# A hybrid decoder layer on one core: the output projection of the first 1024 tokens as eight tiles in a PSUM bank of its own, written out and read back by the norms

## The chip, the cores and the metric

The kernel runs on one core of a Trainium2 chip. The metric is the device time of one launch in microseconds (us): the median of several runs. A profile is one further execution, recorded instruction by instruction; all rows below come from it. The engines are PE (TensorE: matmuls, transposes as matmuls with an identity, and, as PEld, weight loads that overlap them), DVE (VectorE), ACT (ScalarE), POOL (GpSimd) and SP (SyncE, which here only issues DMAs). SBUF is the memory on the core, DRAM the memory outside; PSUM is PE's output memory, eight banks of 128 x 512 f32, which DVE and ACT read ("drain").

## The reference

One layer of a decoder for a prompt of 2048 tokens (width D = 1024) and 32 sample tokens. Cut to what matters here:

```
xn = rmsnorm(x);  [u|q k v f|z xBC dt|B C h] = xn @ W_in
ya = S5(u)        yb = fox attention(q,k,v,f)     # 4 heads x 64, causal, with forget bias
yc = SSD(z,xBC,dt) # Mamba-2, 4 heads, 16 chunks of 128 tokens, a state carried from chunk to chunk
yd = short conv(B,C,h)                            # each of the four is 256 wide and RMS-normed
x  = x + concat(ya,yb,yc,yd) @ W_out              # the output projection
x  = x + relu(rmsnorm(x) @ W_up)^2 @ W_down       # the FFN, 4096 wide
y  = rmsnorm(x)
```

## The kernel before

**Tiles.** The 2048 tokens are four blocks of 512, grouped as `BLOCKS=[(2,3),(0,1)]`: the FFN takes blocks 2 and 3 first and keeps blocks 0 and 1 (the first 1024 tokens) in DRAM until then. Products that need more precision than f16 gives are done three times with high and low f16 halves: x is split into hi and lo, and hi·hi, hi·lo and lo·hi are summed in one PSUM bank.

**The order of the work.** The program is written with a framework that simulates each engine's time line, and by that and by priorities puts all instructions into one fixed list for each engine; the engines run their lists in order, and semaphores make an instruction wait for its inputs or for a free buffer. So an instruction that waits holds up all that stands behind it in its engine's list. Written order is: the input projections (`phase_in`), SSD (`ssd`), attention (`fox`, with another priority, so that its instructions fill in beside SSD), output projection (`outproj`), FFN (`ffn`). In the trace attention's score exponentials run from 746 to 1132 us, SSD's chunks from about 856 to 1048, the output projection's matmuls from 1061 on, and the FFN follows.

**Attention** (`fox`). For each of the four blocks j and each head h, `maxima` makes scores to find the row maxima (tiles `kbm`, `mx`), some steps ahead, and `attend` goes over the 128-key tiles: scores by two matmuls into a "b" bank (`pb<-q,k` and `pb<-q,kba`; the kba and kbm tiles come from DRAM), an exponential on ACT (`P`, L902), its f16 copy on ACT for three tiles of four (`ph`, L906), the remainder on POOL (`pl`), then three matmuls with v for each 128 queries ("AV"), summed in a bank that the head keeps. After the last head of a block `fox_out` norms 128 tokens at a time: a square on ACT (`fo_on`, `fo_ssq`, L956), a scaled copy on ACT (L959), two transposes, and copies to `fo_cat`, which are written to DRAM as the attention quarter of `catD`.

**SSD** (`ssd_prompt`). Sixteen chunks, each with `prepare` (one chunk ahead) and `advance`. Small products through "x" and "d" banks, an exponential `sE`, copies `sBt`, and DVE work between them. After chunks 10, 12, 13 and 14 one fourth of W_out is prepared (`w_out`, `wprep`): 1 MB loaded into `ws`, a square over it on ACT (`wscale`), a scaled f16 copy on ACT and the low half on DVE (`split`).

**PSUM.** One pool of eight banks: two "x", one "d", five "b". Scores and AV go to "b"; SSD uses "x" and "d"; the output projection uses "x" for its products (`px`) and "d" for the norms' transposes (`pd`).

**Output projection** (`outproj`). It goes over pairs of 128-token tiles, 256 tokens each. `load` brings the normed quarters (`cat`, four DMAs, two buffers) and x (1 MB into `x2`). `product` makes 128 tokens x 512 columns by 48 matmuls (128 x 256 each) in an "x" bank, and two DVE instructions (L1907) add it to x2. For blocks 0 and 1 each of four pairs is loaded, gets its eight products of 24 matmuls, and `norm_pair` follows at once: a square on ACT (`xn`), a multiplication on DVE, eight transposes a tile through the one "d" bank, their copies on ACT (`xt`), and `combine`: differences on DVE (`tt`), then f16 hi on ACT and lo on DVE (`hnr`). x2 and hnr are written to DRAM (`xD`, `hD`), from where the FFN takes them later. Then block 2 is loaded and projected (`first`), the pools of attention are closed, block 2's norms follow, and block 3.

Blocks 2's and 3's x2 and those of blocks 0 and 1 share the same two x2 tiles, with one buffer each, so block 2's x can only be loaded when the norms of the pair that was in its tile have read it.

Of the kernel before, what the change touches and what calls it, by code (L numbers as in the profile page):

```python
# [9 lines left out]
F32 = mybir.dt.float32  # L10
F16 = mybir.dt.float16
# [3 lines left out]
OP = mybir.AluOpType  # L15
# [4 lines left out]
D = 1024  # L20
# [7 lines left out]
BLOCKS = [(2, 3), (0, 1)]  # L28
# [75 lines left out]
class K:  # L104
# [29 lines left out]

    def ps(self, tag, shape, name=None, dt=F32):
        g = self.bank.get(tag, "d" if tag == "w" else tag)
        return self.psum.tile(shape, dt, name=name or ("p" + g), tag=g, bufs={"x": 2, "d": 1, "b": 5}[g])

    def mm(self, out, lhsT, rhs, start=True, stop=True):
        self.nc.tensor.matmul(out, lhsT, rhs, start=start, stop=stop, skip_group_check=True)  # L140
# [95 lines left out]
    def run(self):  # L236
        tc = self.tc
        with ExitStack() as ctx:
            self.consts = ctx.enter_context(self.pool("consts", 1))
            self.small = ctx.enter_context(self.pool("small", 2))  # L240
            self.dr = ctx.enter_context(tc.tile_pool(name="dr", bufs=1, space=bass.MemoryType.DRAM))
            self.psum = ctx.enter_context(tc.tile_pool(name="psum", bufs=1, space=bass.MemoryType.PSUM))
            mix = ctx.enter_context(ExitStack())
            self.mixc = mix.enter_context(self.pool("mixc", 1, "right"))
            with ExitStack() as c2:
                bg = self.phase_in(c2)
            self.wst = ctx.enter_context(self.pool("wst", 2))
            self.wp = ctx.enter_context(self.pool("wp", 4))
            first = tc.cur_priority
            tc.cur_priority = first + 50000  # L250
            if "ssd" in self.stages:
                with self.priority(first), self.banks(t="x", s="x", o="d"), ExitStack() as c3:
                    self.mark("ssd")
                    self.ssd(c3)
            if "fox" in self.stages:
                with self.priority(bg):
                    self.mark("fox")
                    self.fox(mix)
            if getattr(self, "dump", None):
                self.dump_cat()  # L260
            with self.banks(mm="x", t="d"):
                self.mark("out")
                self.outproj(ctx, mix)
            if "ffn" in self.stages:
                self.mark("ffn")
                with self.banks(s="x", mm="b", t="d", o="d"):
                    self.ffn()
# [779 lines left out]
    def ssd_prompt(self, ctx, Dp, av, sample):  # L1047


        nc, tc, A, O = self.nc, self.tc, self.A, self.O  # L1050
# [33 lines left out]
        r = p1.tile([15, 640], F32, name="RLc")  # L1084
# [76 lines left out]
        for i in range(NT):  # L1161
            cur, nx = nx, prepare(i + 1) if i + 1 < NT else None
            old = yo
            hT, yo = advance(i, hT, *cur)

            if old is not None:
                self.fox_out(p2, old, 128, i - 1, "t", 2)
            next(sample, None)
            if i in (10, 12, 13, 14):
                next(wo)  # L1170
        for _ in sample:
            pass
# [1 line left out]
        t = self.ps("t", [128, 2, 128])  # L1174
# [105 lines left out]
    def fox_sample(self):  # L1280
# [3 lines left out]
        with ExitStack() as ctx:  # L1284
# [43 lines left out]
            for hp in range(2):  # L1328
                for hf in range(2):
                    ps = slice(hf * 64, hf * 64 + 64)  # L1330
                    nc.vector.tensor_scalar(Qn[ps, hp, 2 * hp + hf, :], p[ps, hp, :], 0.125, None, op0=OP.mult)
# [417 lines left out]
    def s5_scan(self, p1, p2, XS, Pr, Pi, g0, fin):  # L1749
# [7 lines left out]
        for Q, P in ((Qr, Pr), (Qi, Pi)):  # L1757
            for par in range(2):
                ps = slice(par * 64, par * 64 + 64)
                nc.vector.tensor_copy(Q[ps, :, 1], P[ps, par:8:2, 16])  # L1760
# [107 lines left out]
    def w_out(self):  # L1868
        for m in range(4):
# [4 lines left out]
            self.Wo.append((w, f))  # L1874
            yield

    def outproj(self, ctx, mix):

        nc, A = self.nc, self.A
        W = self.Wo  # L1880
        self.fp = ctx.enter_context(self.pool("ffn", 1))
        self.hnp = ctx.enter_context(self.pool("hn0", 1))
        gb, self.ish, g8 = self.gain_row(self.hnp, A["norm_ffn_g"], "ffn", True)

        self.xp = {BLOCKS[0][0]: ctx.enter_context(self.pool("x2a", 1))}
        rot = mix.enter_context(self.pool("rot", 2, "right"))

        self.xD = {b: [self.dr.tile([128, 2 * D], F32, name=f"x2D{b}{i}") for i in range(2)] for b in BLOCKS[1]}
        self.hD = {b: [self.dr.tile([128, 7 * 4 * 2 * 128], F16, name=f"hnD{b}{i}") for i in range(2)] for b in BLOCKS[1]}

        def load(u, b, i):

            cat = self.hnp.tile([128, 8, 2, 256], F16, name="cat", tag="cat", bufs=2)
            for g in range(4):
                nc.sync.dma_start(cat[:, 2 * g:2 * g + 2], self.catD[g][u // 2][:, :, :, u % 2 * 256:u % 2 * 256 + 256])
            x2 = self.xp[b].tile([128, 2, D], F32, name="x2", tag=f"x2{b}{i}")
            nc.sync.dma_start(x2, A["x_prompt"][0, u * 256:(u + 1) * 256, :].rearrange("(i p) d -> p i d", p=128))
            return cat, x2

        def product(cat, x2, i, m):  # L1900

            p = self.ps("mm", [128, 512])
            for mm in range(2):
                self.proj_tok(p[:, mm * 256:(mm + 1) * 256], cat[:, :, :, i * 128:i * 128 + 128], W[m + mm][0], 0, 256)
            for mm in range(2):
                o = x2[:, i, (m + mm) * 256:(m + mm + 1) * 256]
                nc.vector.scalar_tensor_tensor(o, p[:, mm * 256:(mm + 1) * 256], W[m + mm][1], o, op0=OP.mult, op1=OP.add)  # L1907

        for b in BLOCKS[1]:
            for i in range(2):  # L1910
                cat, x2 = load(2 * b + i, BLOCKS[0][0], i)
                for t in range(2):
                    for m in (0, 2):
                        product(cat, x2, t, m)
                hn = rot.tile([128, 7, 4, 2, 128], F16, name="hnr")
                self.norm_pair(x2, gb, hn)
                nc.sync.dma_start(self.xD[b][i], x2.rearrange("p t d -> p (t d)"))
                nc.sync.dma_start(self.hD[b][i], hn.rearrange("p o k a n -> p (o k a n)"))
        first = [load(2 * BLOCKS[0][0] + i, BLOCKS[0][0], i) for i in range(2)]
        for i, t, m in ((i, t, m) for i in range(2) for t in range(2) for m in (0, 2)):  # L1920
            product(*first[i], t, m)
        mix.close()
        self.xp[BLOCKS[0][1]] = ctx.enter_context(self.pool("x2b", 1, "right"))
        self.hp = ctx.enter_context(self.pool("hn", 1))
        self.bank["t"] = "b"
        self.wup = ctx.enter_context(self.pool("wu", 2, "right"))
        self.wts = {}
        self.accs = self.hp.tile([128, 8, NS], F32, name="accs")
        self.wsc = self.hp.tile([128, 2, 4096 // FC, 2], F32, name="wsc")
        self.x2, self.hn = {}, {}  # L1930
        for b in BLOCKS[0]:
            n = 128 + (NS // 4 if b == BLOCKS[0][0] else 0)
            hn = self.hp.tile([128, 2, 7, 4, 2, n], F16, name=f"hn{b}", tag=f"hn{b}")
            prs = first
            if b != BLOCKS[0][0]:
                prs = [load(2 * b + i, b, i) for i in range(2)]

                for i, t, m in ((i, t, m) for m in (0, 2) for i in range(2) for t in range(2)):
                    product(*prs[i], t, m)
            if b == BLOCKS[0][0]:  # L1940
                self.ffn_wu(0, 0)
            for i in range(2):
                self.norm_pair(prs[i][1], gb, hn[:, i, :, :, :, 0:128], b == BLOCKS[0][1])
            if b == BLOCKS[0][0]:
                self.out_sample(hn, g8)
            self.x2[b] = [x2 for _, x2 in prs]
            self.hn[b] = hn
# [357 lines left out]
```

## Time and profile before

| | us |
|---|---|
| median of 3 runs (2593.56 to 2594.98) | 2594.95 |
| the profiled execution, its own time | 2598.28 |
| its span, from the first instruction to the last | 2596.5 |
| mean granted clock of TensorE, share of full | 0.972 |
| busy: PE / DVE / ACT / POOL | 2439.7 / 2010.8 / 1313.2 / 1212.3 |
| output projection's matmuls `px<-w,cat`, 1536 of them, busy | 180.2 |

All times in rows count from the span's start. A busy time is the union of an engine's instructions; the mean of one matmul is its latency in a pipeline and is longer than the distance from one to the next. Idle time before a group of instructions is followed by what ended it. PEclk is the clock that TensorE was granted, as a share of 2.4 GHz.

### The profile page before, as it was taken

How to read it: one execution, taken by the hardware profiler on the slowest of the kernel's cores; microseconds unless marked ns; L12 is line 12 of the kernel's file. 1: busy time of each engine (PE TensorE's matmuls, PEld its weight loads, DVE VectorE, ACT ScalarE, POOL GpSimd, SP SyncE). 2: the span in 40 equal slices, each digit the busy share in tenths (PEclk: the TensorE clock that was granted, in tenths of full speed). 3: DMA queues.
4: the chain of work that ended last, by engine and by line, in shares of the span. 5: the costliest groups of instructions: out<-in, count | busy, mean ns of one | idle time of the engine just before them, and what ended most of it. 6: DMA issues, size and time to landing. Idle time of an engine off the chain costs nothing.

```text
span 2596.5 us, 51309 instructions
## 1 busy us (share of the span) xinstructions
PE 2439.7 (94%) x20496; PEld 1663.5 (64%) x20496; DVE 2010.8 (77%) x3746; ACT 1313.2 (51%) x2449; POOL 1212.3 (47%) x1265
## 2 busy tenths in 40 slices
PE   7989999999999899999979999999998999999997
PEld 6975554454467677689856666666665666666664
DVE  7566667874576777654589998889997898999996
ACT  6534332033346677562455555665556454555554
POOL 3403122223114566550255555656556665666652
PEclk9989999999999998999979999999999999999999
DMA  6333416879632433356111111111135211121201
GB/s 176 102 81 86 99 30 218 302 248 334 224 101 77 136 96 104 101 171 216 52 41 50 51 64 50 49 66 34 62 124 214 74 62 49 53 66 49 66 33 65
DMA packets 209321, 277.78 MB, mean 107 GB/s; under 512 B 42837, under 2 KB 177106, under 8 KB 198810
## 3 DMA queue, kind: packets, MB, share of 16 engines
q1 hardware_dynamic: 195050, 202.65, 25.0%
q0 software_dynamic: 9376, 67.64, 7.2%
q10 hardware_dynamic: 4656, 4.23, 0.5%
q8 instruction: 160, 2.62, 0.4%
q14 instruction: 79, 0.65, 0.1%
HBM read 217.33 MB, written 54.29 MB: 105 GB/s over the span
## 4 chain that ended last, share of the span: by engine, by line
PE 51%; DVE 16%; POOL 13%; DMA 6%; ACT 6%; issue 5%; SPq 1%; POOLq 0%; DVEq 0%; ACTq 0%
PE pb L140 25%; PE px L140 23%; DVE x L2191 4%; DVE wu L177 2%; PE pd L140 2%; DMA kp<-in_cache_v_dram,ptV 1%; DVE wd L177 1%; PE pb L144 1%; POOL ht L2146 1%; POOL ws L2037 1%; POOL ht L2148 1%; DVE wdT L177 1%; POOL ws L2039 1%; POOL ws L2038 1%; POOL ws L2036 1%
## 5 line engine op out<-in xcount | busy, mean ns | idle before, releaser
L140 PEld LDWEIGHTS <-wu 128*128 128x128 f16 x5376 | 530.3, 99 | 222.9 <-issue 37.3
L2191 DVE SCALAR_TENSOR_TENSOR x<-pb,ff,x 128x512 f32<-128x512 f32 x840 | 591.3, 740 | 27.3 <-PE pb L140 23.3
L140 PE MATMUL px<-hn,wu 128*128 128x256 f16 (+1 forms) x3072 | 428.0, 276 | 14.6 <-DVE hn L1981 7.0
L140 PEld LDWEIGHTS <-ht 128*128 128x128 f16 x2712 | 264.5, 99 | 231.6 <-issue 26.0
L140 PE MATMUL pb<-wdT,ht 128*128 128x512 f16 x1440 | 379.8, 381 | 15.8 <-DVE x L2191 9.2
L140 PE MATMUL px<-xT,w 128*128 128x512 f16 (+1 forms) x1968 | 371.9, 341 | 1.5 <-ACT da L731 1.2
L140 PE MATMUL pb<-wd,ht 128*128 128x512 f16 x1272 | 336.8, 381 | 6.1 <-DVE x L2191 5.2
L140 PE MATMUL pb<-hn,wu 128*128 128x256 f16 (+1 forms) x2304 | 303.6, 277 | 15.8 <-DVE x L2191 7.6
L140 PEld LDWEIGHTS <-w 128*128 128x128 f16 x2160 | 168.6, 99 | 188.1 <-issue 30.9
L909 POOL TENSOR_TENSOR pl<-P,ph 128x512 f16<-128x512 f32 (+3 forms) x160 | 166.9, 1053 | 155.5 <-ACT ph L906 59.6
L176 ACT ACTIVATE wu<-ws,wsc 128x1024 f16<-128x1024 f32 (+1 forms) x128 | 129.4, 1036 | 130.8 <-POOL ws L2039 76.7
L140 PE MATMUL px<-w,cat 128*128 128x256 f16 x1536 | 180.2, 274 | 3.4 <-DMA cat<-cat 3.3
L177 DVE SCALAR_TENSOR_TENSOR wu<-ws,wsc,wu 128x1024 f16<-128x1024 f32 (+1 forms) x128 | 168.6, 1331 | 18.0 <-ACT wu L176 17.7
L140 PEld LDWEIGHTS <-cat 128*128 128x128 f16 x1536 | 149.6, 98 | 25.7 <-DMA cat<-cat 3.4
L140 PE MATMUL px<-w,xT 128*128 128x128 f16 (+1 forms) x2400 | 156.1, 225 | 10.2 <-DVE v L576 4.5
L140 PEld LDWEIGHTS <-xT 128*128 128x128 f16 (+1 forms) x2672 | 153.1, 101 | 15.5 <-issue 5.5
L902 ACT ACTIVATE P<-pb,nck,cc 128x512 f32<-128x512 f32 (+3 forms) x160 | 112.2, 710 | 75.4 <-PE pb L140 69.7
L2143 ACT ACTIVATE ht<-fr 128x1024 f16<-128x1024 f32 (+1 forms) x60 | 64.2, 1070 | 159.9 <-POOL fr L2149 159.9
L2146 POOL TENSOR_TENSOR ht<-fr,ht 128x512 f16<-128x512 f32 (+1 forms) x60 | 84.2, 1403 | 113.0 <-ACT ht L2145 113.0
L2062 POOL TENSOR_TENSOR ws<-ws 128x512 f32<-128x512 f32 x30 | 41.1, 1371 | 187.1 <-DVE wd L177 187.1
L871 DVE TENSOR_REDUCE mx<-pb 128x1 f32<-128x512 f32 (+3 forms) x160 | 94.8, 607 | 40.0 <-PE pb L140 38.9
L2120 ACT ACTIVATE fr<-fr 128x256 f32<-128x256 f32 (+1 forms) x192 | 77.0, 414 | 90.5 <-DVE fr L2101 89.7
(717 smaller groups left out, 4647.1 us busy)
## 6 DMA issues: line engine op xcount, KB each, us to landing
ws<-in_w_up_dram SPq DMA_DIRECT2D x32, 1024.0 KB
ws<-in_w_down_dram SPq DMA_DIRECT2D x32, 1024.0 KB
ws<-in_w_in_dram SPq DMA_DIRECT2D x22, 512.0 KB
x<-in_x_prompt_dram SPq DMA_DIRECT2D x16, 512.0 KB
cat<-cat SPq DMA_DIRECT2D x32, 256.0 KB
x<-in_x_prompt_dram SPq DMA_DIRECT2D x8, 1024.0 KB
out_y_prompt_dram<-x SPq DMA_DIRECT2D x32, 256.0 KB
hnD<-hnr SPq DMA_DIRECT2D x4, 1792.0 KB
```

The costliest lines, as they stand in the source:

```text
L140: self.nc.tensor.matmul(out, lhsT, rhs, start=start, stop=stop, skip_group_check=True)
L144: self.nc.tensor.transpose(out, in_, self.ident[:n, :n])
L176: self.nc.scalar.activation(hi, x, AF.Copy, scale=sc)
L177: self.nc.vector.scalar_tensor_tensor(lo, x, sc, hi, op0=OP.mult, op1=OP.subtract)
L871: nc.vector.tensor_reduce(mx[:, ii, jb:jb + 1], s[:, :n], axis=AX.X, op=OP.max)
L902: nc.scalar.activation(P[:, :n], s[:, :n], AF.Exp, bias=nck[:, j, h, kt:kt + 1], scale=cc[:, h // 2:h // 2 + 1])
L909: (nc.gpsimd if 1 else nc.vector).tensor_sub(pl[:, :n], P[:, :n], ph[:, :n])
L2062: nc.gpsimd.tensor_sub(B11, B12, B11)
L2120: nc.scalar.activation(x, x, AF.Relu)
L2143: nc.scalar.activation(ht[:, o:o + m, 0, :], x, AF.Copy)
L2146: nc.gpsimd.tensor_sub(ht[:, 0:2, 1, :], C[:, 0:2, :], ht[:, 0:2, 0, :])
L2191: nc.vector.scalar_tensor_tensor(o, p, f, o, op0=OP.mult, op1=OP.add)
```

## The change

- PSUM: the "b" group is a pool of its own. It has five banks during `phase_in` and again after attention's pools are closed; during SSD and attention it has four, and a new group "e" has one.
- Blocks 0 and 1 are no longer projected in `outproj`. A new function `out_tile` is called eight times, for 128 tokens each, after `fox` in the written order and before `outproj`: it loads the tile's four quarters (`ecat`, four DMAs, two buffers) and x (`ex2`), makes two products of 48 matmuls through the "e" bank, adds them on DVE (four instructions), and writes x2 to `xD`.
- In `outproj` the four pairs' norms then read the sums back from `xD` into x2 (one DMA of 1 MB a pair); the pair's load, products and the write of xD are gone there. The norms themselves, hD, block 2 and block 3 are as before.
- W_out is prepared after SSD chunks 0, 1, 2 and 3 instead of 10, 12, 13 and 14.

```diff
     def ps(self, tag, shape, name=None, dt=F32):
         g = self.bank.get(tag, "d" if tag == "w" else tag)
-        return self.psum.tile(shape, dt, ..., tag=g, bufs={"x": 2, "d": 1, "b": 5}[g])
+        pool, n = self.banks_of[g]
+        return pool.tile(shape, dt, name=name or ("p" + g), tag=g, bufs=n)
...
-            self.psum = ctx.enter_context(tc.tile_pool(name="psum", ...))
+            self.banks_of = {}
+            self.psum_groups(ctx, x=2, d=1)
...
             with ExitStack() as c2:
+                self.psum_groups(c2, b=5)
                 bg = self.phase_in(c2)
...
+            self.psum_groups(mix, b=4, e=1)
...
+            eop = eo.enter_context(self.pool("eo", 2))
...                                   # ssd and fox stand here
+            for b in BLOCKS[1]:
+                for t in range(4):
+                    self.out_tile(eop, b, t)
+            eo.close()
...
-            if i in (10, 12, 13, 14):
+            if i < 4:
                 next(wo)
...
+    def out_tile(self, pool, b, t):
+        nc, A, W = self.nc, self.A, self.Wo
+        cat = pool.tile([128, 8, 2, 128], F16, name="ecat")
+        for g in range(4):
+            nc.sync.dma_start(cat[:, 2 * g:2 * g + 2], self.catD[g][b][:, :, :, t * 128:t * 128 + 128])
+        x2 = pool.tile([128, D], F32, name="ex2")
+        r = (4 * b + t) * 128
+        nc.sync.dma_start(x2, A["x_prompt"][0, r:r + 128, :])
+        for m in (0, 2):
+            p = self.ps("e", [128, 512])
+            for mm in range(2):
+                self.proj_tok(p[:, mm * 256:(mm + 1) * 256], cat, W[m + mm][0], 0, 256)
+            for mm in range(2):
+                o = x2[:, (m + mm) * 256:(m + mm + 1) * 256]
+                nc.vector.scalar_tensor_tensor(o, p[:, mm * 256:(mm + 1) * 256], W[m + mm][1], o, op0=OP.mult, op1=OP.add)
+        nc.sync.dma_start(self.xD[b][t // 2][:, t % 2 * D:t % 2 * D + D], x2)
...
         for b in BLOCKS[1]:
             for i in range(2):
-                cat, x2 = load(2 * b + i, BLOCKS[0][0], i)
-                for t in range(2):
-                    for m in (0, 2):
-                        product(cat, x2, t, m)
+                x2 = self.xp[BLOCKS[0][0]].tile([128, 2, D], F32, name="x2", tag=f"x2{BLOCKS[0][0]}{i}")
+                nc.sync.dma_start(x2.rearrange("p t d -> p (t d)"), self.xD[b][i])
                 hn = rot.tile([128, 7, 4, 2, 128], F16, name="hnr")
                 self.norm_pair(x2, gb, hn)
-                nc.sync.dma_start(self.xD[b][i], x2.rearrange("p t d -> p (t d)"))
                 nc.sync.dma_start(self.hD[b][i], hn.rearrange("p o k a n -> p (o k a n)"))
...
         mix.close()
+        self.psum_groups(ctx, b=5)
```

How the lists change at three places. In these rows a line stands for an instruction in its engine's list, `out<-in`, with its size and, after x, how many follow each other; the changed kernel's line numbers are 7 to 33 higher at the same code.

ACT, the early chunks of SSD (the `sE` and `sBt` of one chunk). `w,w_ss<-ws` is the square over a fourth of W_out, `w<-ws,w_sc` its scaled copy. The changed kernel:

```order
L190 ACTIVATE w,w_ss<-ws 128x8x256
L979 ACTIVATE fo_on<-syo,fo_rs 128x256
L1130 ACTIVATE sE<-px 128x512
L183 ACTIVATE w<-ws,w_sc 128x8x256
L922 ACTIVATE P<-pb,nck,cc 128x256
L922 ACTIVATE P<-pb,nck,cc 128x128
L1140 ACTIVATE sBt<-px 128x256
```

The kernel before, at the same chunk:

```order
L1110 ACTIVATE sE<-px 128x512
L479 ACTIVATE fo_cat<-pb,gcat 128x128
L956 ACTIVATE fo_on,fo_ssq<-fo_o 128x256
L479 ACTIVATE fo_cat<-pb,gcat 128x128
L956 ACTIVATE fo_on,fo_ssq<-fo_o 128x256
L1120 ACTIVATE sBt<-px 128x256
```

W_out's squares and copies have moved here, between one chunk's `sE` and `sBt`; all four fourths are prepared between chunks 3 and 5.

ACT at the end of attention; `xn`, `xt` and `hnr` belong to the norms of blocks 0 and 1, `fo_on` and `fo_cat` to attention's own norm. The changed kernel:

```order
L926 ACTIVATE ph<-P 128x128
L2013 ACTIVATE hnr<-tt 128x16x128
L2000 ACTIVATE xt<-pd 128x512 x2
L1992 ACTIVATE xn,n_ssq<-x_16876 128x1024
L2013 ACTIVATE hnr<-xt 128x8x128
L976 ACTIVATE fo_on,fo_ssq<-fo_o 128x256 x2
L2000 ACTIVATE xt<-pd 128x512
L979 ACTIVATE fo_on<-fo_o,fo_rs 128x256 x2
L2000 ACTIVATE xt<-pd 128x512
L1992 ACTIVATE xn,n_ssq<-x_16876 128x1024
```

The kernel before:

```order
L906 ACTIVATE ph<-P 128x128
L1980 ACTIVATE hnr<-tt 128x16x128
L1959 ACTIVATE xn,n_ssq<-x_16146 128x1024
L956 ACTIVATE fo_on,fo_ssq<-fo_o 128x256 x2
L959 ACTIVATE fo_on<-fo_o,fo_rs 128x256 x2
L479 ACTIVATE fo_cat<-pb,gcat 128x128
L956 ACTIVATE fo_on,fo_ssq<-fo_o 128x256
L479 ACTIVATE fo_cat<-pb,gcat 128x128
```

The norms' copies `xt` and `hnr` of blocks 0 and 1 now stand among and ahead of attention's last squares and copies.

PE at the same place: `pd<-cst,xn` are the norms' transposes, `pb<-cst,fo_on` those of attention's norm, `px<-w,cat` the output projection of `outproj`. The changed kernel:

```order
L147 LDWEIGHTS pl
L147 MATMUL pb<-v_3_11148,pl 128x65
L151 MATMUL pd<-cst,xn 128x128 x12
L151 MATMUL pb<-cst,fo_on 128x128 x4
L151 MATMUL pd<-cst,xn 128x128 x4
L151 MATMUL pb<-cst,fo_on 128x128 x4
L151 MATMUL pd<-cst,xn 128x128 x8
L147 LDWEIGHTS cat
L147 MATMUL px<-w,cat 128x256
```

The kernel before:

```order
L140 LDWEIGHTS cat
L140 MATMUL px<-w,cat 128x256
L144 MATMUL pd<-cst,xn 128x128 x4
L140 LDWEIGHTS cat
L140 MATMUL px<-w,cat 128x256
L140 LDWEIGHTS cat
L140 MATMUL px<-w,cat 128x256
L140 LDWEIGHTS cat
L140 MATMUL px<-w,cat 128x256
L144 MATMUL pb<-cst,fo_on 128x128 x2
```

Before, the projection's matmuls of blocks 0 and 1 stood between these transposes; now they stand earlier, and the transposes come one behind another.

## Rows read from the trace of the kernel before

**Rows 1.** The page, busy time of each engine (us, share of span, instructions)

```profile
PE 2439.7 (94%) x20496; PEld 1663.5 (64%) x20496; DVE 2010.8 (77%) x3746; ACT 1313.2 (51%) x2449; POOL 1212.3 (47%) x1265
```

**Rows 2.** Windows; columns: us, PE, PEld, DVE, ACT, POOL busy, PEclk, DMA, GB/s

```profile
855.00:875.00 20.00, 18.07 (x176) 12.79 (x177) 13.77 (x31) 13.36 (x24) 10.33 (x13) 1.00 0.42 131
875.00:1048.00 173.00, 163.04 (x1595) 123.16 (x1593) 135.08 (x306) 125.36 (x274) 119.84 (x160) 0.94 0.35 98
1048.00:1062.00 14.00, 10.45 (x119) 6.34 (x117) 9.75 (x25) 9.89 (x18) 9.57 (x10) 0.93 0.55 142
1060.00:1070.00 10.00, 8.62 (x84) 6.45 (x85) 3.64 (x12) 2.62 (x4) 2.30 (x3) 0.66 0.87 266
1062.00:1146.00 84.00, 81.49 (x980) 64.14 (x979) 45.24 (x78) 52.13 (x89) 49.84 (x50) 0.97 0.34 114
1146.00:1240.00 94.00, 94.00 (x862) 84.82 (x863) 44.84 (x69) 31.67 (x52) 9.82 (x18) 1.00 0.61 211
```

**Rows 3.** Chain that ended last, 1048 to 1245 (start us, us, what)

```profile
1054.55 6.79 DMA cat<-cat
...
1206.34 33.42 PE px L140 x306
```

**Rows 4.** PE's groups, 1062 to 1146 (busy us, mean ns, idle before, releaser)

```profile
L140 PE MATMUL px<-w,cat 128*128 128x256 f16 x349 | 47.2, 278 | 0.0
...
L140 PE MATMUL pb<-q,kba 74*128 74x512 f16 x31 | 12.0, 389 | 0.9 <-DMA kba<-kb 0.9
```

**Rows 5.** ACT's groups, 1050 to 1215

```profile
L902 ACT ACTIVATE P<-pb,nck,cc 128x512 f32<-128x512 f32 x38 | 28.6, 776 | 19.3 <-PE pb L140 15.4 <-POOL pl L909 3.9
L906 ACT ACTIVATE ph<-P 128x512 f16<-128x512 f32 x27 | 16.6, 631 | 0.9 <-PE pb L140 0.5
L1967 ACT ACTIVATE xt<-pd 128x512 f32<-128x512 f32 x16 | 9.5, 597 | 32.9 <-PE pd L144 32.9
L1959 ACT ACTIVATE xn<-x 128x1024 f32<-128x1024 f32 x9 | 9.4, 1046 | 3.2 <-DVE x L1907 3.2
L1980 ACT ACTIVATE hnr<-tt 128x2048 f16<-128x2048 f32 x4 | 7.6, 1910 | 8.9 <-DVE tt L1976 8.9
L1980 ACT ACTIVATE hnr<-xt 128x1024 f16<-128x1024 f32 x4 | 4.2, 1062 | 0.1
...
L1980 ACT ACTIVATE hnr<-xt 128x512 f16<-128x512 f32 x4 | 2.5, 634 | 0.1
L959 ACT ACTIVATE fo_on<-fo_o,fo_rs 128x256 f32<-128x256 f32 x4 | 2.0, 510 | 2.7 <-POOL fo_rs L151 2.7
...
L1959 ACT ACTIVATION_READ_ACCUMULATOR xn<-x 128x1 f32 x9 | 1.7, 189 | 0.0
L902 ACT ACTIVATE P<-pb,nck,cc 128x256 f32<-128x256 f32 x3 | 1.7, 565 | 0.8 <-PE pb L140 0.8
...
L906 ACT ACTIVATE ph<-P 128x256 f16<-128x256 f32 x3 | 1.2, 413 | 0.1
```

**Rows 6.** DVE's groups, 1050 to 1215

```profile
L1907 DVE SCALAR_TENSOR_TENSOR x<-px,wo_f,x 128x256 f32<-128x256 f32 x38 | 16.7, 477 | 8.6 <-PE px L140 8.6
...
L1981 DVE TENSOR_TENSOR hnr<-tt,hnr 128x2048 f16<-128x2048 f32 x4 | 9.2, 2292 | 6.3 <-ACT hnr L1980 6.3
```

**Rows 7.** Tile ws, 840 to 1060 (count: least/median/most ns, first to last start)

```profile
L160 SPq DMA_DIRECT2D ws<-in_w_out_dram x4: 388/392/497, 844.0 to 1009.0; - x4
L183 ACT ACTIVATE w<-ws x4: 1899/1902/1910, 852.9 to 1019.0; 128x2048 f16<-128x2048 f32 x4
...
L176 ACT ACTIVATE w<-ws,w_sc x4: 1989/1998/2002, 976.6 to 1026.2; 128x2048 f16<-128x2048 f32 x4
L177 DVE SCALAR_TENSOR_TENSOR w<-ws,w_sc,w x4: 2341/2343/2353, 978.7 to 1029.3; 128x2048 f16<-128x2048 f32 x4
```

**Rows 8.** Tile cat: SP's time to issue its DMAs

```profile
L1895 SPq DMA_DIRECT2D cat<-cat x32: 518/626/2539, 1054.5 to 1241.7; - x32
```

More of the change, by code (lines that the diff above doesn't have):

```diff
@@ L136, in ps, with psum_groups @@
         g = self.bank.get(tag, "d" if tag == "w" else tag)
-        return self.psum.tile(shape, dt, name=name or ("p" + g), tag=g, bufs={"x": 2, "d": 1, "b": 5}[g])
+        pool, n = self.banks_of[g]
+        return pool.tile(shape, dt, name=name or ("p" + g), tag=g, bufs=n)
+    def psum_groups(self, ctx, **groups):
+        pool = ctx.enter_context(self.tc.tile_pool(name="psum_" + "".join(groups), bufs=1, space=bass.MemoryType.PSUM,
+                                                   reuse_waits="tile"))
+        self.banks_of.update({g: (pool, n) for g, n in groups.items()})
     def mm(self, out, lhsT, rhs, start=True, stop=True):
@@ L241, in run @@
             self.dr = ctx.enter_context(tc.tile_pool(name="dr", bufs=1, space=bass.MemoryType.DRAM))
-            self.psum = ctx.enter_context(tc.tile_pool(name="psum", bufs=1, space=bass.MemoryType.PSUM))
+            self.banks_of = {}
+            self.psum_groups(ctx, x=2, d=1)
             mix = ctx.enter_context(ExitStack())
@@ L248, in run @@
             self.wp = ctx.enter_context(self.pool("wp", 4))
+            self.psum_groups(mix, b=4, e=1)
+            self.xD = {b: [self.dr.tile([128, 2 * D], F32, name=f"x2D{b}{i}") for i in range(2)] for b in BLOCKS[1]}
+            self.hD = {b: [self.dr.tile([128, 7 * 4 * 2 * 128], F16, name=f"hnD{b}{i}") for i in range(2)] for b in BLOCKS[1]}
+            eo = ctx.enter_context(ExitStack())
+            eop = eo.enter_context(self.pool("eo", 2))
             first = tc.cur_priority
@@ L260, in run @@
                 self.dump_cat()
+            self.mark("outproj_tiles")
+            for b in BLOCKS[1]:
+                for t in range(4):
+                    self.out_tile(eop, b, t)
+            eo.close()
             with self.banks(mm="x", t="d"):
@@ L1886, in outproj @@
         rot = mix.enter_context(self.pool("rot", 2, "right"))
-        self.xD = {b: [self.dr.tile([128, 2 * D], F32, name=f"x2D{b}{i}") for i in range(2)] for b in BLOCKS[1]}
-        self.hD = {b: [self.dr.tile([128, 7 * 4 * 2 * 128], F16, name=f"hnD{b}{i}") for i in range(2)] for b in BLOCKS[1]}
         def load(u, b, i):
```

## The prediction

> **What bounds the kernel now.** I read the page's busy line first: PE works 94% of the span, the next engine 77% [rows 1]. So time falls only where PE waits, or where it runs at a low clock. Then the windows of the stretch that the change touches, from SSD's second chunk to block 2's last product, 875 to 1240 us [rows 2]. There the reader should take PE's idle time (window less busy) and the clock for each part: SSD 173 − 163.0 = 10.0 idle at .94; the gap at 1048 3.6 idle at .93; attention with the projection 2.5 idle at .97; the projection alone 0.0 idle at 1.00. Idle is 16.0 in all. The clock costs .06 x 173 + .07 x 14 + .03 x 84 = 13.9, of which I take 2 as counted twice (a low clock while PE is idle anyway). So of 365 us some 28 are lost and 337 are work. The chain shows the single large piece: 6.8 us in which all wait for the projection's first `cat` [rows 3]. After 1146 PE runs without a pause, and nothing that is only moved gains there.
>
> The chain has one more row that I need: 306 matmuls, most of them of the projection, in 33.42 us [rows 3], so .109 us from one to the next. (The .278 mean of the group is latency [rows 4].)
>
> **What is removed, added and moved.** The number of matmuls stays: blocks 0 and 1 are 768 of the 1536 before and after. DVE's two additions per product stay (.477 each [rows 6]). Only where they stand is new, so the gain can be no more than the 28 us that PE loses now, less what the new order makes it wait.
>
> *Before the last out_tile matmul.* By PE's new list 327 of the 768 stand before SSD's last matmul (35.6 us of work) and 441 among attention. PE's work from 875 to the last of them is 337 less what comes behind it (67.1, below), 270 us. How much is lost on top, call it r? Below, 0: the new matmuls fill every pause and the clock stays up. Above, 28: all pauses stay, because they are waits within SSD's chain of chunks and a matmul put between them only moves them. SSD's part loses about 18 of the 28 (10.0 idle, 10.4 clock, less the 2). I take half of it, 9, since the filling covers PE's idle time but not the waits in the list's order. Attention with out_tile matmuls loses 2.5 + 2.5 in 84 us in the nearest row [rows 2], so 4 for the some 70 us after SSD. r = 13.
>
> *The gap at 1048.* `cat`'s load before the first product goes; the tiles' loads are of 128 tokens and are asked for a tile or two ahead. What is late next is in the next paragraph.
>
> *Behind the last out_tile matmul.* Here a wait is new. PE has left: 240 matmuls with v, 44 of scores, 52 transposes, and block 2's first two products, 96 matmuls. The 1062 to 1146 window gives the price: 349 px x .109 = 38.0 leave 43.5 us for 631 others, .069 each. So 336 x .069 + 96 x .109 = 33.7 us. Then both "x" banks are full, and the third product needs the first one's drain. That drain is in DVE's list behind the low half of a pair's `hnr`, and this behind ACT's `hnr` of the same pair; ACT's list up to there holds, from the first exponential whose score stands behind the last out_tile matmul [rows 5]:
> - 13 full P x .776 and 6 smaller x .565: 13.5
> - 9 full ph x .631 and 6 smaller x .413: 8.2
> - 6 squares of the norms x (1.046 + .189): 7.4
> - 8 xt x .597: 4.8
> - two times the three hnr, 1.062 + .634 + 1.910: 7.2
> - 9 squares and copies of attention's norm at about .51: 4.6
>
> That is 45.7 us of ACT's own work in one line. It begins some 1.5 us after the last out_tile matmul (two pairs of scores, four matmuls x .389 [rows 4]). Behind it DVE needs 2.29 + 2 x .48 = 3.3 [rows 6]. So the third product starts not before 50.5 us, where PE has 33.7 us to do: it waits 17 us. Behind it on PE are block 2's other six products (288 matmuls and 18 to 20 transposes, 33.4 us as in rows 3). In the kernel before these norms stood beside 768 matmuls of the projection and cost PE nothing (ACT busy 31.7 of 94 us after 1146 [rows 2]). After a wait PE starts slow: in 1060 to 1070, behind the wait for `cat`, the granted clock was .66, between the levels of 1.2 and 2.4 GHz [rows 2]. At that row 10 us cost 3.4; I add 3.4. The wait is on ACT and so cannot go below 0; it could be 0 if ACT's list runs ahead of PE there, which the exponentials, fed by PE, don't allow, and 17 is what the rows give.
>
> The Trainium skill bears on this wait ("TensorE: Matmul & The Clock Gate", section "HAM oscillation — how this bites in real kernels"): a kernel whose PE waits between bursts of matmuls starts each burst throttled and pays for the change of clock every time. The .66 after one wait of some 7 us [rows 2, 3] agrees. By the rule the 3.4 is due for this one new wait, and would be due again for each one I have not seen.
>
> *The sum.* 270 + 13 + 1.5 + 45.7 + 3.3 + 33.4 + 3.4 = 370.3 against 365: +5.3 us. The profiled execution took 2598.28 (span 2596.5 and 1.8 around it); its sum is 2603.6. It lies 3.3 over the median, so the median becomes 2594.95 + 5.3 = 2600.
>
> *Edits with a price of 0.* W_out's preparation is moved, not changed: four squares x 1.90, copies x 2.00, low halves x 2.34 [rows 7]. It leaves 976 to 1029 and comes into the chunks from 3 on; I take it as even, and price the other answer under the rivals. Scores have four banks instead of five: PE uses the fifth only when ACT is over three steps late; 0, at worst 62 score banks of the last heads x .2 = 12 (the time by which a bank, held for .78 of P and its scores .39 x 2, comes back later than the next step asks). One "e" bank: a product must wait for the two drains of the one before, .95, so 16 x .95 = 15 if PE had nothing between; its list has attention or SSD between most, so 0 to 3, held in r. SP gets 28 more DMAs at .626 [rows 8], 17.5 us of issue over 200; PE, which waits for `kba` .9 us now [rows 4], would see them as a later `kba`, between 0 and those few us. x2's trip to `xD` and back: 1 MB a pair, where four pairs' x came before; even.
>
> On the one "e" bank the same section of the Trainium skill states that adding PSUM double-buffering gave no further gain in its kernel. By it a second bank would be worth nothing and the single one costs 0; by the rows it may cost up to 15. No row here shows a single bank under products of this size, so both ends stand in the range.
>
> **Rivals.**
> *The filling gains more than I allow* (.21). r = 13 is a guess between bounds. If SSD's waits are filled (327 matmuls are 35.6 us, twice what SSD loses) and the clock stays at 1.00, r is 3, and the time at which PE has work left shrinks too: the copies from 976 on no longer stand in SSD's way. Then 360.3, −5; with half of the 17-us wait hidden, because ACT at 52 of 84 us busy [rows 2] has begun its list earlier, −11 to −14. Against it: ACT's work cannot start before its scores. Time: 2584.
> *The wait is half as long* (.14): the squares and hnr of one pair are done beside the last out_tile matmuls, so 8 us of ACT's list fall before them. Then about −3: 2592, no difference that can be measured.
> *W_out's early preparation stalls SSD* (.20, with the banks). ACT gets 4 x (1.90 + .19 + 2.00) = 16.4 us and DVE 9.4 into some 25 us in which they are busy at the 13.4 and 13.8 of 20 that the 855 row shows [rows 2]. Free are 8.3 and 7.8, so ACT is 8.1 too late, between `sE` and `sBt`, for which SSD's chunk and all PE work behind it in the list wait; with a restart at the low clock about +10 on top of my sum: 2610. It decides from the point where ACT's free time in the two chunks is below 16.4. For it: DVE and ACT stand in one chain with PE in a chunk. Against: attention's exponentials in the list may stand further apart there, and 976 to 1029 becomes free.
> *The change doesn't do what it says*: excluded; PE's list has the 327 matmuls within SSD.
>
> **How the numbers follow.** The forecast, +5.3, has .45; its own range, −2 to +14, comes from r between 6 and 22. What this kernel's runs can tell from no change is 0.2%, 5.2 us, so 2589.8 to 2600.2 is the same. The forecast lies at that edge: .20 of its .45 the same, .25 slower. With the rivals: faster .21; same .20 + .14 = .34; slower .25 + .20 = .45. The range goes from the first rival's time, 2584, to the forecast's r at its bound of 28 or to the W_out rival with a late bank, 2594.95 + 23: 2618.
>
> **What would show it.** Right: in the profile after, PE is idle for 10 to 25 us between attention's last matmul and block 2's third product, and what ends it is DVE's drain of `px`, behind ACT's `hnr`. The windows of SSD show less idle PE per us than 10.0 in 173 and a clock over .94. The first wait for `cat` is gone. Wrong: the wait isn't there, or is at block 2's `cat` or x load; or PE waits in chunks 3 to 5 for ACT's `sE` or `sBt` with W_out's copies ahead of them; or the "e" bank's drain ends many short waits. From the end of block 2's products on the two traces should be alike, with FFN shifted as a whole; if it isn't, my sum has left something out.

## The result and the profile after

The changed kernel takes 2618.98 us (median of 4 runs, 2618.59 to 2619.46) against 2594.26 for the kernel before in the same runs: 1.0096 times, 95% interval 1.0079 to 1.0114, so 24.7 us slower. The forecast was slower by 5.3, with 2618 as the upper end of its range; the way was right, the size was not. Single runs of the kernel before spread from 2585 to 2603 in the experiments below, so a difference of a few us between two kernels is read from medians with their intervals, not from two profiles.

The page of the changed kernel, busy time of each engine; it answers to [rows 1]:

```profile
PE 2439.5 (93%) x20496; PEld 1659.3 (63%) x20496; DVE 2011.3 (77%) x3746; ACT 1322.0 (51%) x2449; POOL 1219.8 (47%) x1265
```

PE's work is the same to .2 us; the 20.6 us by which the span grew (2617.1 against 2596.5) are PE's idle time. Windows of the changed kernel, with the columns of [rows 2]:

```profile
820.00:900.00 80.00, 63.38 (x534) 43.86 (x534) 52.88 (x126) 44.93 (x81) 37.78 (x46) 0.84 0.54 158
875.00:1050.00 175.00, 167.74 (x1649) 131.95 (x1647) 113.92 (x274) 105.51 (x225) 101.84 (x136) 0.97 0.37 102
1050.00:1158.00 108.00, 106.15 (x1163) 81.66 (x1162) 51.86 (x116) 57.58 (x101) 50.16 (x54) 1.00 0.39 114
1158.00:1222.00 64.00, 42.37 (x448) 31.07 (x447) 38.79 (x57) 45.62 (x86) 36.33 (x45) 0.79 0.43 143
1222.00:1258.00 36.00, 36.00 (x314) 31.74 (x314) 24.30 (x35) 15.73 (x24) 3.53 (x7) 0.95 0.84 297
```

The row from 1158 to 1222 is the loss: 21.6 us idle and a clock of .79 in 64 us. The two rows above it (875 to 1050 and 1050 to 1158) are what the change does well: 7.3 us idle in 175 at .97, where SSD before had 10.0 in 173 at .94, and 1.9 in 108 at 1.00. The first row, which holds most of W_out's preparation, is bad: 16.6 us idle at .84. The same window in the trace before, and the one where W_out stood then:

```profile
820.00:900.00 80.00, 70.42 (x767) 51.42 (x765) 57.64 (x139) 54.33 (x124) 43.36 (x59) 0.96 0.44 127
1000.00:1050.00 50.00, 44.34 (x369) 32.80 (x369) 36.69 (x86) 36.11 (x73) 31.89 (x38) 0.81 0.26 70
```

9.6 us idle at .96 from 820 to 900. The kernel before loses its part later: 5.7 us idle at .81 from 1000 to 1050, where the changed kernel has no idle time at all (50.00 of 50.00 at 1.00).

What ends the waits in the bad stretch: PE's waits between 1150 and 1270 in the changed kernel (who waited, for whom, us in total, times, longest), and then those of SP's DMA queue from 1100 to 1260:

```profile
PE pb L147 <- POOL pl L929: 5.8, 5, 1.9
PE pb L151 <- ACT fo_on L979: 5.4, 3, 4.2
PE px L147 <- DMA cat<-cat: 5.2, 1, 5.2
PE pd L151 <- ACT xt L2000: 4.5, 4, 2.1
```

```profile
...
SPq L1947 <- DVE xn L1995: 19.7, 2, 18.1
SPq L1932 <- DVE xn L1995: 15.7, 2, 9.7
...
SPq L392 <- DMA x2D<-ex: 4.8, 1, 4.8
```

The chain of the changed kernel in the same stretch (start us, us, what):

```profile
1157.77 0.78 PE pe L147 x7
1158.57 0.89 DVE ex L1912 x2
1159.47 5.12 DMA x2D<-ex
1164.61 0.36 SPq L392
...
1165.48 4.40 DMA cat<-cat
1169.93 2.74 PE px L147 x12
...
1221.42 0.48 DVE x L1942
1221.94 4.99 PE px L147 x27
```

L392 loads the gain row for the norms. It waits until the last out_tile tile has been written out, and block 2's `cat` stands behind it on SP: that chain, 1159.5 to 1169.9, takes the place of the wait at 1054 [rows 3]. PE still had scores and products with v until 1164.7 and then stood for 5.2 us. In PE's list the scores that attention's exponentials still need stand behind block 2's first matmuls, so ACT stood longer than PE, 10.3 us, up to 1176.8 (time line of ACT; start us, us, what, then the idle time before it and what ended it):

```profile
1176.77 1.45 ACT L922 ACTIVATE P<-pb,nck,cc 128x512 f32<-128x512 f32 x2 [10.34 <-PE pb L147]
```

Then comes the wait that was forecast, to 1221.9, the start of block 2's third product. What released block 2's first drain last is not ACT's `hnr` (the low half on DVE was done by 1219.6) but the load of block 2's x, 1.2 us later (time line of DVE). SP could issue that load (L1932 above) only when the norms had read the tile:

```profile
1221.01 1.66 DVE L1942 SCALAR_TENSOR_TENSOR x<-px,wo_f,x 128x256 f32<-128x256 f32 x4 [1.17 <-DMA x<-in_x_prompt_dram]
```

Why everything of the norms stands there: tile `ecat`'s matmuls, the loads of tile `x` (up to 1300) and tile `xn`'s squares (up to 1300) in the changed kernel, with least/median/most ns and first and last start:

```profile
L147 PE MATMUL pe<-w,ecat x768: 269/273/422, 873.2 to 1158.3; 128*128 128x256 f16 x192
...
L1947 SPq DMA_DIRECT2D x<-x2D x4: 332/470/1450, 1064.5 to 1202.3; - x4
...
L1992 ACT ACTIVATE xn<-x x13: 1040/1050/1078, 1161.1 to 1297.8; 128x1024 f32<-128x1024 f32 x13
```

The first pair's sums are read back from 1064.5 on, but the first square comes at 1161.1, behind the last out_tile matmul at 1158.3. My reading is that SBUF lies between: the pool of the out_tile tiles is closed ahead of `outproj`, and the next pools opened, `xn`'s and that of the gain row and `cat`, get its place. No row shows an address; what shows it so far is that L392 waits for the last tile's `x2D<-ex`, and the experiments test it.

### The profile page after: what moved, and what is told of

Its sections match the earlier page's. It is cut to its first block, busy times and chain, and to the rows that moved or that the text cites. A ratio compares the mean times of both kernels' runs of the same rounds, so it can differ in the third digit from the quotient of the medians.

```text
span 2617.1 us, 51331 instructions
## 1 busy us (share of the span) xinstructions
PE 2439.5 (93%) x20496; PEld 1659.3 (63%) x20496; DVE 2011.3 (77%) x3746; ACT 1322.0 (51%) x2449; POOL 1219.8 (47%) x1265
## 4 chain that ended last, share of the span: by engine, by line
PE 54%; DVE 15%; POOL 11%; DMA 7%; ACT 6%; issue 5%; SPq 1%; POOLq 0%; DVEq 0%; ACTq 0%
PE pb L147 25%; PE px L147 22%; DVE x L2224 3%; PE pe L147 3%; DVE wu L184 2%; PE pd L147 2%; DMA ws<-in_w_up_dram 2%; DVE wd L184 1%; POOL ws L2070 1%; PE pb L151 1%; DMA kp<-in_cache_v_dram,ptV 1%; ACT wu L183 1%; POOL ws L2072 1%; DVE s5cat L500 1%; POOL ws L2069 1%
## 5 line engine op out<-in xcount | busy, mean ns | idle before, releaser
L147 PE MATMUL px<-hn,wu 128*128 128x256 f16 (+1 forms) x3072 | 428.5, 276 | 20.6 <-ACT fr L2131 10.2
L2153 ACT ACTIVATE fr<-fr 128x256 f32<-128x256 f32 (+1 forms) x192 | 77.2, 413 | 97.4 <-DVE fr L2134 96.7
L2179 POOL TENSOR_TENSOR ht<-fr,ht 128x512 f16<-128x512 f32 (+1 forms) x60 | 72.1, 1202 | 114.1 <-ACT ht L2178 111.2
L147 PE MATMUL pe<-w,ecat 128*128 128x256 f16 x768 | 104.9, 277 | 2.1 <-DVE w L184 1.6
L2154 ACT ACTIVATE fr<-fr 128x256 f32<-128x256 f32 (+1 forms) x256 | 102.8, 413 | 4.2
```

Of the source, the lines that this page charges most:

```text
L2153: nc.scalar.activation(x, x, AF.Relu)
L2154: nc.scalar.activation(x, x, AF.Square)
L2179: nc.gpsimd.tensor_sub(ht[:, 0:2, 1, :], C[:, 0:2, :], ht[:, 0:2, 0, :])
```

## Experiments

My theory after the result: (a) the norms of blocks 0 and 1 cannot start before the last out_tile tile, because their tiles lie in its SBUF, and so stand in one lump with no matmuls beside them; (b) block 2's `cat` waits likewise, and the two waits add up. Rivals: the smaller number of score banks, the single "e" bank, or W_out's early place.

Every ratio below is to the kernel before on the same chip, whose medians were 2592.7 in the first four runs, 2594.0 in the next four and 2592.4 in the last.

**cat_free**

```diff
+        self.xp = {BLOCKS[0][0]: ctx.enter_context(self.pool("x2a", 1))}
         self.fp = ctx.enter_context(self.pool("ffn", 1))
         self.hnp = ctx.enter_context(self.pool("hn0", 1))
...
-        self.xp = {BLOCKS[0][0]: ctx.enter_context(self.pool("x2a", 1))}
```

> The changed kernel with one edit: in outproj the pool of the two x2 tiles is opened first, so that it, and not the norms' xn, the gain row and block 2's cat, takes the SBUF that the out_tile tiles leave. Theory (two waits that add up: block 2's cat load cannot begin before the last out_tile tile is written out, some 10 us, and the norms of blocks 0 and 1 stand in one lump behind it, some 20 us): the first of the two goes, the second stays, since the norms now wait for the x2 tiles; 2606 to 2610, 9 to 13 us under the changed kernel. Rival 1 (the cat wait only overlaps the lump of ACT work): 2616 to 2620. Rival 2 (fewer score banks or the single e bank cost the time all along): 2616 to 2620.

Measured: 2618.03, 1.0086 [1.0073, 1.0099]. None of PE's waits from 1150 to 1270 is for `cat` any more, and nothing is won that can be told from noise: theory (b) fell, and the time is in the range of the rivals. Tiles `ecat`, `x` and `xn` of this kernel:

```profile
L147 PE MATMUL pe<-w,ecat x768: 269/272/421, 878.2 to 1175.8; 128*128 128x256 f16 x192
...
L1947 SPq DMA_DIRECT2D x<-x2D x4: 319/320/343, 1177.8 to 1208.6; - x4
...
L1942 DVE SCALAR_TENSOR_TENSOR x<-px,wo_f,x x26: 470/475/484, 1225.2 to 1299.0; 128x256 f32<-128x256 f32 x26
```

Since `cat` comes early, the list has block 2's first two products and attention ahead of the last out_tile tile, which now ends at 1175.8, 17.5 us later (5.0 of these are there at the first one, 878.2 against 873.2, where PE's list is still the same); the lump starts there, and block 2's first drain is at 1225.2 (after: 1221.0). From the last out_tile matmul to that drain it is 49.4 us, where I had reckoned 50.5 to the third product, two drains of .48 later; in the changed kernel it is 62.7, with ACT's 10.3 us in it. So in these two traces block 2's third product comes at the end of the last out_tile tile plus the lump: what the lump lost by `cat` in one, the last out_tile tile lost by standing later in the other.

**xn_free**

```diff
+        self.catp = ctx.enter_context(self.pool("catp", 1))
         self.fp = ctx.enter_context(self.pool("ffn", 1))
...
-            cat = self.hnp.tile([128, 8, 2, 256], F16, name="cat", tag="cat", bufs=2)
+            cat = self.catp.tile([128, 8, 2, 256], F16, name="cat", tag="cat", bufs=2)
```

(the two later users of the tag "cat" take it from the same pool)

> The changed kernel with one edit: a pool that holds only the cat tiles is opened first in outproj, so that the cat tiles take the SBUF of the out_tile tiles, and xn, the gain row and the x2 tiles lie elsewhere. Theory: the norms of blocks 0 and 1 no longer wait for the last out_tile tile; the wait of PE behind attention (about 15 us idle and 5 at a low clock in the changed kernel) goes, the wait for cat stays or is shortened: 2595 to 2603. Rival 1 (ACT is the bound in any order, so the norms' ACT work only comes back as a wait elsewhere): 2612 to 2620. Rival 2 (banks): 2616 to 2620.

Measured: 2596.02, 1.0004 [.9993, 1.0015]: the loss is gone, to within what can be told, by the places of tiles in SBUF alone. Tiles `xn` and `ecat`, and PE's waits from 1050 to 1260:

```profile
L147 PE MATMUL pe<-w,ecat x768: 269/272/421, 872.1 to 1155.9; 128*128 128x256 f16 x192
...
L1993 ACT ACTIVATE xn<-x x16: 1039/1058/1078, 1069.4 to 1295.5; 128x1024 f32<-128x1024 f32 x16
```

```profile
PE pb L147 <- POOL pl L929: 7.6, 11, 1.2
PE px L147 <- DMA cat<-cat: 1.0, 1, 1.0
...
PE pd L151 <- ACT xt L2001: 0.2, 1, 0.2
```

The first square is at 1069.4 instead of 1161.1. The waits for `fo_on` are gone, those for `xt` fall from 4.5 to .2 and that for `cat` from 5.2 to 1.0. The last out_tile matmul starts at 1155.9 against 1158.3, so nothing else has become much faster. Theory (a) is shown, and the rivals fall as causes of the loss: the banks and W_out's early place are the same here. With the loss gone, what is left of the change cannot be told from nothing.

**half and half_xn_free**

```diff
-            for b in BLOCKS[1]:
+            for b in BLOCKS[1][:1]:
                 for t in range(4):
                     self.out_tile(eop, b, t)
...
+                if b == BLOCKS[1][0]:
                     # x2 read back from xD, as in the changed kernel
+                else:
+                    cat, x2 = load(2 * b + i, BLOCKS[0][0], i)   # and its eight products,
...                                                              # and xD written, as before
```

> The changed kernel, but only block 0 (512 tokens) goes through out_tile; block 1 is loaded, projected and normed in outproj as in the kernel before. Theory (the lump of norms costs because no matmuls are left beside it): 384 matmuls, 42 us of PE work, stand beside the norms again and the cat wait has the scores beside it: 2595 to 2606. Rival 2 (banks, which are the same here): 2612 to 2620.

> Both: only block 0 through out_tile, and the cat tiles' pool first in outproj. Theory: SSD's pauses are filled and neither wait is left; 2583 to 2595, at or below the kernel before. Rival 1 (SSD's pauses were not what the time hangs on): 2594 to 2600. Rival 2 (banks): above 2605.

Measured: half 2592.84, .9996 [.9985, 1.0007]; half_xn_free (with the edit of xn_free) 2598.07, 1.0016 [1.0004, 1.0027]. Tiles `ecat` and `xn` of half:

```profile
L147 PE MATMUL pe<-w,ecat x384: 269/273/421, 873.2 to 1070.9; 128*128 128x256 f16 x192
...
L2000 ACT ACTIVATE xn<-x x16: 1040/1056/1078, 1075.5 to 1291.3; 128x1024 f32<-128x1024 f32 x16
```

The loss is gone here as well; the last matmul of the projection starts at 1286.6 against 1310.4 in the changed kernel and 1292.6 before. But half does two things at once: 384 matmuls stand beside the norms again, and the last out_tile matmul is at 1070.9 instead of 1158.3, so the norms' place in SBUF is free 87 us earlier. Either would do by (a), and the run does not split them. It does exclude the banks, which are as in the changed kernel. It also shows why the two remedies don't add up: in half_xn_free the first square is at 1076.7 against 1075.5, so there is nothing left for the places in SBUF to win. Half came out below its range of 2595 to 2606, and half_xn_free above its 2583 to 2595; its median is 5 us over half's, the intervals overlap by a little, and why stays open (its profile is 6 us behind half's at the first out_tile matmul already, 879.3 against 873.2).

**b_wo_early and b_4banks**: the kernel before with one part of the change each.

```diff
-            if i in (10, 12, 13, 14):
+            if i < 4:
                 next(wo)
```

```diff
-        return self.psum.tile(..., bufs={"x": 2, "d": 1, "b": 5}[g])
+        return self.psum.tile(..., bufs={"x": 2, "d": 1, "b": 4}[g])
```

> The kernel before with one edit: W_out prepared after SSD chunks 0 to 3. Theory (the move is even: in the changed kernel PE loses some 29 us, idle and low clock, between 820 and 900 where the kernel before loses 13, and the kernel before loses 15 more between 1000 and 1050): same as before within 0.2%, 2588 to 2598. Rival (the early place is dearer, since ACT and DVE are fuller there and the late place has attention beside it): 2598 to 2608.

> The kernel before with four b banks instead of five throughout (the eighth PSUM bank unused). Theory: the fifth bank is worth little; 2592 to 2600 (here also the input phase and the FFN have one bank less, so this is an upper bound). Rival (attention's scores and the heads' sums need five): 2600 to 2615.

Measured: b_wo_early 2605.61, 1.0053 [1.0034, 1.0072]; b_4banks 2713.11, 1.0460 [1.0438, 1.0482], far outside both of its ranges. W_out's early place is not even: alone it costs 11.6 us, as the rival had it. Two windows of b_wo_early show the price at the new place, 9.4 us idle at .76 (before: 5.0 at .98), and that at the old one only a part is given back, 2.6 idle at .93 instead of 5.7 at .81:

```profile
850.00:900.00 50.00, 40.58 (x290) 30.88 (x288) 34.66 (x82) 34.91 (x67) 25.89 (x37) 0.76 0.49 148
...
1000.00:1050.00 50.00, 47.44 (x457) 35.85 (x454) 37.13 (x94) 35.36 (x87) 32.52 (x49) 0.93 0.25 65
```

b_4banks tells by its trace more than by its time. The projection's matmuls there, from first to last start:

```profile
L140 PE MATMUL px<-w,cat x1536: 269/273/422, 1019.9 to 1290.0; 128*128 128x256 f16 x192
```

The last one, at 1290.0, is no later than in the two traces of the kernel before (1292.6 and 1289.3). So up to the end of the projection four banks cost nothing that shows; the 119 us are lost behind it, in the FFN, where the changed kernel has its fifth bank again. There PE waits longer for the drains; the largest of its waits from 1290 to the end, of b_4banks and then of the kernel before:

```profile
PE pb L140 <- DVE x L2191: 63.0, 42, 2.3
```

```profile
PE pb L140 <- DVE x L2191: 22.0, 21, 4.4
```

**xn_wo and half_wo**: xn_free and half with W_out prepared after chunks 3, 5, 7 and 9 (`if i in (3, 5, 7, 9)`).

> xn_free with W_out prepared after SSD chunks 3, 5, 7 and 9 instead of 0 to 3. Theory (four preparations in some 40 us stop SSD, spread over 80 us they find room on ACT and DVE; the out_tile matmuls still fill the rest): 6 to 12 us under xn_free, 2583 to 2590. Rival (what is saved at the start comes back, because the out_tile matmuls start later and stand among attention): 2592 to 2600.

> half with W_out prepared after SSD chunks 3, 5, 7 and 9. Theory: as for xn_wo, 6 to 12 us under half: 2581 to 2588. Rival: 2590 to 2598.

Measured: xn_wo 2607.13, 1.0053 [1.0034, 1.0072]; half_wo 2596.19, 1.0019 [1.0002, 1.0036]. Both expectations of a gain failed; half_wo lies in its rival's range, and xn_wo is even 11 us above xn_free, beyond its rival's range too. PE's waits from 1140 to 1210 show only a little of it: xn_wo has 3.7 us for `cat` and 3.5 for `P`, where xn_free has 1.0 and .6, but xn_free has 4.7 for `pl` where xn_wo has 1.0, and in sum it is 8.2 against 7.1. xn_wo's waits are few and long, xn_free's many and short, and the clock differs: .87 from 1150 to 1200 in xn_wo (first row), 1.00 in xn_free (second).

```profile
1150.00:1200.00 50.00, 42.41 (x457) 30.64 (x456) 27.30 (x40) 35.80 (x58) 30.96 (x31) 0.87 0.45 145
```

```profile
1150.00:1200.00 50.00, 44.82 (x514) 33.39 (x512) 37.81 (x48) 39.04 (x63) 36.33 (x30) 1.00 0.61 201
```

By these rows .13 x 50 = 6.5 us at most are lost to the clock there, an estimate that counts the pauses in; the rest is not split.

**half_wo_first and xn_wo_first**: half and xn_free with W_out prepared ahead of the first chunk.

```diff
+        for _ in range(4):
+            next(wo)
         nx = prepare(0)
...
-            if i < 4:
-                next(wo)
```

> half (block 0 through out_tile, block 1 in outproj) with all four fourths of W_out prepared ahead of SSD's first chunk. Theory (W_out's ACT and DVE work costs PE time where it stands inside SSD's chunks; ahead of them ACT is busy only 18 of 50 us, at 700 to 750): 4 to 10 us under half, 2583 to 2590, and under the kernel before. Rival (it only delays SSD's start): 2590 to 2600.

> xn_free with W_out prepared ahead of SSD's first chunk. Theory as for half_wo_first: 2585 to 2592. Rival: 2594 to 2604.

Measured: half_wo_first 2587.59, .9987 [.9974, 1.0000]; xn_wo_first 2597.34, 1.0017 [1.0003, 1.0031]. half_wo_first has the lowest median of the study, 4.8 us under the kernel before and within its range, but its interval reaches 1.0000: about the .2% that a measurement can tell. Its interval also overlaps with half's, and xn_wo_first, in its rival's range, is no better than xn_free: that W_out is cheaper ahead of SSD is not shown.

**wo_late**: the changed kernel with W_out back after chunks 10, 12, 13 and 14.

> The changed kernel with one edit: W_out prepared after SSD chunks 10, 12, 13 and 14, as before, so that no out_tile matmul can stand within SSD's first 10 chunks. Theory (the lump of norms behind the last out_tile tile is the loss, and the early W_out only pays for itself by the matmuls that fill SSD): the lump stays, SSD is unfilled; 2612 to 2628. Rival (the early W_out is the loss): 2595 to 2606.

Measured: 2620.20, 1.0107 [1.0087, 1.0128], as the theory had it. Tiles `ecat` and `xn`:

```profile
L147 PE MATMUL pe<-w,ecat x768: 269/272/418, 966.2 to 1166.0; 128*128 128x256 f16 x192
```

```profile
L1992 ACT ACTIVATE xn<-x x13: 1042/1052/1076, 1171.0 to 1297.4; 128x1024 f32<-128x1024 f32 x13
```

The out_tile matmuls start 93 us later, W_out's early price is gone with the filling that it allowed, and the loss is the same: the first square still stands behind the last out_tile matmul. Two things change at once here, so this run alone does not price them; but the loss stays without the early place, and in xn_free it goes with the early place kept. So W_out's early place, dear by itself, is not what made the changed kernel slower.

**before_again**: the kernel before.

> The kernel before once more, for a second profile: its profiled execution took 3.3 us more than the median of its runs, and it should show where. If the difference is spread, no stretch is off by more than 2 us; if it is in the stretch of the change, the projection's last matmul starts 3 us under 1292.6.

Its span is 2590.9, 5.6 under the first profile's, and the projection's last matmul starts at 1289.3, 3.3 earlier. That is not lost in the stretch of the change: the projection's first matmul is 3.5 earlier already, 1057.9 against 1061.4. The rest lies in the FFN. So the profile on which I reckoned was itself some 4 us above the median of the kernel before.

## Why the prediction was wrong

**What bounds the kernel, and what can be gained: right.** PE was the bound, and its number of matmuls and its busy time didn't change.

**Before the last out_tile matmul: right in sum, in part by luck.** I had 270 us of work and r = 13, so the last out_tile matmul at 1158; it started at 1158.3. But r is the balance of two things that I did not price apart: SSD filled better than I allowed (950 to 1050 without a pause), and W_out's early place, which I priced at 0 and put with .20 under the rivals, costs 11.6 alone (b_wo_early). That the two balance to .3 us is luck.

**The gap at 1048: here it failed.** "`cat`'s load before the first product goes ... What is late next is in the next paragraph": the sum put nothing for a further wait. Late next was `cat` again, at block 2's first product, since it and the gain row had to wait for the SBUF of the last out_tile tile. The sum had ACT's line begin 1.5 us after the last out_tile matmul and run without a stop. It stopped for 10.3 us, up to 1176.8: PE stood at `cat` from 1164.7 to 1169.9, and the scores that feed ACT's next exponentials are behind block 2's first matmuls. So the third product started at 1221.9 and not at 1158.3 + 50.5 = 1208.8: 13.1 late, of which ACT's stop is 10.3.

**The wait behind the last out_tile matmul: right in place and size, nearly in its releasers, wrong in its cause.** The lump of ACT work was reckoned at 45.7 and the way to the third product at 50.5; cat_free, which has no wait for `cat` in it, took 49.4 to block 2's first drain, so some 50.4 to the third product. The last 1.2 us of it, in both traces, are for block 2's x and not for `hnr`; a late x load is one of the signs of being wrong that the prediction names, but a small one here. I took the wait as given by the list's order. xn_free shows that the order itself came from SBUF: with `xn` and the gain row elsewhere the same scheduler puts the first square 92 us earlier, and some 23 of the 24.7 us are gone. So both waits, the one at `cat` and the lump, hang on the same thing, which the prediction does not have: `xn`, the gain row and `cat` lie where the out_tile tiles lay. The pools that are opened where another was closed were in the diff (`eo.close()` just ahead of `outproj`), and I read them for space only, not for waits.

**Behind it.** 33.4 us from the third product to block 2's last was the estimate; 1221.9 to 1257.6 are 35.7. The sum would have had the end of block 2 at 1245.3; it came 12.3 later. Some 3 us more are lost in the FFN (20.6 of span at the end against 17.6 at 1257.6 by the before trace's 1240); where, stays open. The last 4 us are the profiled execution before, 2598.28, which lay that much above the median, while that after, 2618.9, did not. 5.3 + 12.3 + 3.0 + 4 = 24.6, against 24.7 measured.

**Restart at a low clock.** 3.4 us was the term. In the 64 us from 1158 to 1222 the clock was .79 in the mean, .77 in the ten behind the wait for `cat`, though PE was busy throughout, and from 1210 to 1220 PE's few matmuls ran at .50, the level of 1.2 GHz:

```profile
1170.00:1180.00 10.00, 10.00 (x85) 7.43 (x86) 5.88 (x12) 3.01 (x5) 2.40 (x3) 0.77 0.91 272
...
1200.00:1210.00 10.00, 3.91 (x19) 2.48 (x19) 7.93 (x10) 6.36 (x11) 5.15 (x7) 0.60 0.70 263
1210.00:1220.00 10.00, 4.32 (x17) 2.62 (x16) 7.72 (x11) 8.22 (x19) 4.39 (x9) 0.50 0.31 118
```

There were two stretches of waiting, and the clock fell in both. The rule of the Trainium skill on bursts that each start throttled ("TensorE: Matmul & The Clock Gate", section "HAM oscillation — how this bites in real kernels") agrees with these rows. What the low clock cost by itself was not split off.

**One "e" bank, four "b" banks: right.** In front of the out_tile products PE's waits in the changed kernel name W_out's low half (1.6 us) and a norm of the samples (.5), and no drain of the bank; b_4banks shows no delay by 1290 for the four. On the single bank the Trainium skill's remark that double-buffering PSUM gave no further gain (same section) stood nearer than my upper bound of 15.

**Rivals.** That the filling gains more than allowed: half true, for SSD, and hidden behind the lump. That the wait is half as long: no. W_out: true as a price, 11.6 instead of 10, but not what moved the time (wo_late, xn_free).

## What to carry to other kernels

When a pool is closed and others opened behind it, look up which new tiles fall on its SBUF and when each is first needed; put there what is needed last. Work that is filled into an earlier stage takes the cover from what stood beside it in the later one: count what is left beside that. Here moving half of it cost nothing and gained nothing that can be told, and moving all of it, with the pools in the order of xn_free, did no better. A wait in front of a serial lump need not be worth its own length: in cat_free the wait went, the list moved other work ahead of the lump, and the time stayed.

## What was unexpected

One PSUM bank fewer for the scores costs nothing that shows up to the end of the projection and 119 us in a whole program whose FFN uses the same group of banks (b_4banks). And two profiles of the kernel before differed by 5.6 us in span (2596.5 and 2590.9), more than the .2% on which chances were put.
